# A hybrid decoder trunk on one core: the FFNs' gated values are transposed by VectorE and put in place through DRAM

## The chip, the cores and the metric

The kernel runs on one core of a Trainium2 chip. A core has engines with queues of their own: TensorE (PE, matmuls; PEld is its weight load), VectorE (DVE), ScalarE (ACT), GpSimd (POOL) and SyncE (SP), and 16 DMA engines that serve the DMAs which the engines' queues issue. Each queue runs its instructions in the order in which they stand; an instruction that waits holds all behind it. The metric is the time of one execution on the device, in microseconds.

## The reference

Two layers, on 256 tokens of width 1024, all in float32:

```
h += 1/2 * swiglu(rms_norm(h, ffn1_norm), w_gate, w_up, w_down)
h += W_out(sum of four gated token mixers of rms_norm(h))
h += cross_attention(rms_norm(h), rms_norm(mem))
h += 1/2 * swiglu(rms_norm(h, ffn2_norm), w_gate, w_up, w_down)
after the last layer: rms_norm(h, final_norm)

def swiglu(x, w_gate, w_up, w_down):
    return (jax.nn.silu(x @ w_gate) * (x @ w_up)) @ w_down
```

The change concerns the four FFNs (`swiglu`, hidden width 2816), the start of the first of them, and the final norm.

## The kernel before

Tokens are two blocks of 128 (`NB`), `b0` and `b1`. A float32 product is made of three products of rounded parts: weights are split in `wh` and `wl`, activations in `xh` and `xl` (or `hid`'s two parts), and TensorE adds wh·xh, wh·xl and wl·xh.

*Weights.* They come in chunks of 1 MB, four k-tiles of 128 x 512 columns. For each chunk `fetch` (L331) issues one load from SyncE's queue into `wr` (L343, three buffers), then in two halves ScalarE's rounding cast to `wh` (L350) and VectorE's residual `wl` (L351). `linear` (L367) uses a chunk with 24 matmuls: 12 for b0, 12 for b1, each 12 as four of wh·xh, four of wh·xl, four of wl·xh. So a first half of a cast serves the first two of every four.

*An FFN* (`ffn`, L538). The gate and up columns lie in 11 groups of 256 + 256 columns, each group two chunks; the first call of `linear` takes groups 0 and 1 together, in the order g0, g1, g0, g1 (chunks 0 to 3). At the end of a group, `evac` (L554) gates each block: ScalarE's Silu `sg` (L557), VectorE's product `toks` (L558), 128 tokens x 256 values. `hidden` (L541) then has TensorE transpose the four 128x128 squares into a PSUM bank `ht` (L547), and `split` (L364, L365) makes of it `hid`, hidden dimension on the partitions. After the 22 chunks of gate and up come 12 of the down product, which reads `hid`.

*The order.* TensorE's order is that of the program: work put off with `yield n` in a generator (`start`, `tick`) is taken up n half chunks later, so a group's transposes stand half a chunk to a chunk after its last matmul. The order of the other engines is made by a planner when the program is built, and is then fixed. `issue_after(x)` keeps an instruction behind x on its engine.

*The start.* The first chunks are loaded in pieces, then `arrive` (L1248) loads `h`. `tables` (L571) runs in the first FFN: it loads `pos`, `cst` and `bcs` from ScalarE's queue, makes sine tables `tab` (L608, L609) of angles `ang` that VectorE works out of `pos`, and a relative bias (`ge` and `bias`, L642, L644), whose parts fill VectorE through the first layer.

*The end.* `finish_` (L1218) makes, block by block, the second half's square sum on ScalarE, the variance `fvar` and GpSimd's power `rfin`, and scales the halves on ScalarE and VectorE (L1230, L1232).

Of the kernel before, what the change touches and what calls it, by code (L numbers as in the profile page):

```python
# [11 lines left out]
F32 = mybir.dt.float32  # L12
# [7 lines left out]
P = 128  # L20
# [132 lines left out]
def program(tc, a, out, upto="all"):  # L153
# [12 lines left out]
    fp = sb("fp", 2)  # L166
    sp = sb("sp", 4)
    mp = sb("mp", 11)
    lin = ctx.enter_context(tc.tile_pool(name="lin", bufs=4, space=PSUM))
    aux = ctx.enter_context(tc.tile_pool(name="aux", bufs=4, space=PSUM))  # L170
    ctx.enter_context(tc.manual_schedule(engines={mybir.EngineType.PE}))
# [364 lines left out]
        return evac  # L536

    def ffn(xT, nxt):  # L538
        hid = {}

        def hidden(g, toks):  # L541
            yield 2
            t4 = m4("hid", F32R).rearrange("p (s f t) -> p s f t", s=2, f=2)
            ps = bank("ht").rearrange("p (f t) -> p f t", f=2)
            for b in range(NB):
                for k in range(2):
                    pe.transpose(ps[:, k, blk(b)], toks[:, b, k * P:(k + 1) * P], ident)  # L547
            split(t4[:, 0], t4[:, 1], ps)
            hid[g] = t4

        def group(g):
            toks = f2("toks", "toks", 3).rearrange("p (b t) -> p b t", b=2)

            def evac(b, ps):  # L554
                nonlocal paced
                sg = fp.tile([P, 256], F32, tag="sg", name="sg")
                act.activation(sg, ps[:, :256], AF.Silu, scale=xT.r[:, b:b + 1])  # L557
                paced = dve.scalar_tensor_tensor(toks[:, b], ps[:, 256:], xT.r[:, b:b + 1], sg, ALU.mult, ALU.mult)  # L558
                if b == NB - 1:
                    start(hidden(g, toks))  # L560

            return evac

        linear(KD, 512, xT, [group(0), group(1)])
        for g in range(2, 11):
            linear(KD, 512, xT, [group(g)])
        for c in range(2):
            linear(KF, 512, lambda part, k: hid[k // 2][:, part, k % 2, :], [add_to_h(c, 0.5, nxt, 1 if c else 5)])


    def tables():  # L571
# [3 lines left out]
        with tc.issue_after(last.ins):  # L575
            act.dma_start(posi, a["pos"])
            act.dma_start(cst, a["consts"][:, P:CO["dec"][0]])
            act.dma_start(bcs, a["bcols"])
        act.activation(sel, C("sel")[:16], AF.Copy)
        yield 4  # L580
        for o, b, n in ((0, 0, 128), (128, 1, 256)):
            pool.tensor_tensor(reli[:, o:o + n], posi[:, b:b + 1].to_broadcast([P, n]), posi[:, NB:NB + n], ALU.subtract)
        dve.tensor_copy(relt, reli)
# [633 lines left out]
    def finish_(fn):  # L1217
# [3 lines left out]
        for b in range(NB):  # L1221
            square_sum(h[b][0], ss[:, b:b + 1])
            dve.tensor_tensor(t[b][:, :512], h[b][0], fn[:, :512], ALU.mult)
            dve.tensor_scalar(part[:, b:b + 1], ss[:, b:b + 1], 1.0 / D, EPS, ALU.mult, ALU.add)
        for b in range(NB):
            square_sum(h[b][1], ss[:, 2 + b:3 + b])
            v, r = small("fvar", 1), small("rfin", 1)
            dve.scalar_tensor_tensor(v, ss[:, 2 + b:3 + b], 1.0 / D, part[:, b:b + 1], ALU.mult, ALU.add)
            pool.tensor_tensor(r, v, mhalf[:, :1], ALU.pow)
            act.activation(t[b][:, :512], t[b][:, :512], AF.Copy, scale=r)  # L1230
            act.dma_start(out[blk(b), :512], t[b][:, :512])
            dve.scalar_tensor_tensor(t[b][:, 512:], h[b][1], r, fn[:, 512:], ALU.mult, ALU.mult)  # L1232
            nc.sync.dma_start(out[blk(b), 512:], t[b][:, 512:])

    def dump():
# [11 lines left out]

    def arrive():  # L1248
        yield 1
        for c in range(2):  # L1250
            for b in range(NB):
                nc.sync.dma_start(h[b][c], a["x"][b, :, c * 512:(c + 1) * 512])
# [41 lines left out]
```

## Time and profile before

| | |
|---|---|
| time, median of 3 runs | 1585.56 us (1585.09 to 1585.72) |
| the profiled execution | 1585.53 us |
| its span, first to last instruction | 1583.4 us |
| mean granted TensorE clock | 0.998 of full speed |
| busy: TensorE, VectorE, ScalarE | 1572.2, 1065.2, 830.2 us |
| `ht` on TensorE | 176 transposes, 26.3 us busy |
| casts `wh`, residuals `wl` | 536 each, 533.2 and 624.7 us busy |
| moved by DMA | 284.73 MB, 43153 packets, 4784 of them under 512 B |

Matmuls overlap in the pipeline, so the busy times of single ones add up to more than the time that they take in a row; the distance from start to start is what counts. A bracket after an instruction gives the time that the engine stood idle before it and the instruction that ended this.

### The profile page before, as it was taken

What the parts mean: (1) busy time and instruction counts of PE and PEld (TensorE: products, weight loads), DVE (VectorE), ACT (ScalarE), POOL (GpSimd) and SP (SyncE); (2) the same over time, 40 slices, a digit from 0 to 9 for tenths busy, and PEclk for the clock granted to TensorE, in tenths of its full rate; (3) what the DMA queues carried; (4) which work ended last, traced back from release to release, by engine and by line L of the source; (5) the groups of instructions that cost most, each with busy time, mean ns of one, the idle gap of its engine ahead of it and who ended that gap; (6) DMA issues with size and microseconds to landing.
All of it is one profiled execution on the core that took longest, in us unless ns stands there. A gap on an engine that the chain in (4) does not pass through costs nothing.

```text
span 1583.4 us, 20797 instructions
## 1 busy us (share of the span) xinstructions
PE 1572.2 (99%) x8208; PEld 1345.1 (85%) x8208; DVE 1065.2 (67%) x1704; ACT 830.2 (52%) x1236; POOL 26.0 (2%) x40
## 2 busy tenths in 40 slices
PE   9999999999999999999999999999999999999998
PEld 7888889898888988888888888898988899888886
DVE  5887699997787656554565546697656766565543
ACT  6744446566655545444454444475575555554443
POOL 0000000000000000000000000000000000000000
PEclk9999999999999999999999999999999999999999
DMA  7655544444655444555555556444546554455552
GB/s 291 239 180 179 194 169 160 165 164 144 212 214 177 169 160 163 187 182 182 191 188 188 183 176 209 151 159 157 184 149 237 186 186 164 156 182 176 191 174 74
DMA packets 43153, 284.73 MB, mean 180 GB/s; under 512 B 4784, under 2 KB 5168, under 8 KB 11056
## 3 DMA queue, kind: packets, MB, share of 16 engines
q1 hardware_dynamic: 40464, 276.12, 51.3%
q10 hardware_dynamic: 2592, 7.29, 1.4%
q8 instruction: 64, 1.05, 0.3%
q14 instruction: 33, 0.27, 0.0%
HBM read 282.34 MB, written 1.05 MB: 179 GB/s over the span
## 4 chain that ended last, share of the span: by engine, by line
PE 98%; DMA 1%; ACT 0%; DVE 0%; issue 0%; POOLq 0%; POOL 0%; ACTq 0%
PE lin L393 77%; PE lin L411 11%; PE tr L422 2%; PE ht L547 1%; PE xo L1191 1%; PE lin L381 1%; PE xs L1145 1%; DMA bcs<-bcols 1%; PE up L953 1%; PE my L869 0%; PE ds L1038 0%; PE ms L989 0%; PE pt L680 0%; DMA pcs<-pcols 0%; ACT wh L350 0%
## 5 line engine op out<-in xcount | busy, mean ns | idle before, releaser
L351 DVE TENSOR_TENSOR wl<-wr,wh 128x1024 fp32r<-128x1024 f32 (+3 forms) x536 | 624.7, 1191 | 375.1 <-ACT wh L350 372.7
L350 ACT ACTIVATE wh<-wr 128x1024 fp32r<-128x1024 f32 (+3 forms) x536 | 533.2, 1030 | 493.4 <-PE lin L393 381.7
L393 PE MATMUL lin<-wh,xh 128*128 128x512 f32 (+1 forms) x1200 | 328.5, 395 | 1.1 <-ACT wh L350 0.9
L393 PE MATMUL lin<-wl,xh 128*128 128x512 f32 (+1 forms) x1200 | 320.7, 389 | 0.6 <-DVE wl L351 0.6
L393 PE MATMUL lin<-wh,xl 128*128 128x512 f32 (+1 forms) x1200 | 320.4, 389 | 0.0
L393 PEld LDWEIGHTS lin<-wl,xh 128*128 128x128 f32 x1200 | 225.1, 188 | 48.0 <-DVE wl L351 1.4
L393 PEld LDWEIGHTS lin<-wh,xl 128*128 128x128 f32 x1200 | 225.3, 188 | 47.0
L393 PEld LDWEIGHTS lin<-wh,xh 128*128 128x128 f32 x1200 | 219.2, 188 | 43.7 <-ACT wh L350 2.2
L393 PE MATMUL lin<-wh,hid 128*128 128x512 f32 x704 | 176.0, 390 | 0.0
L393 PEld LDWEIGHTS lin<-wh,hid 128*128 128x128 f32 x704 | 131.6, 188 | 27.1
L393 PE MATMUL lin<-wl,hid 128*128 128x512 f32 x352 | 95.4, 389 | 0.0
L393 PEld LDWEIGHTS lin<-wl,hid 128*128 128x128 f32 x352 | 66.1, 188 | 13.9
L557 ACT ACTIVATE sg<-lin,rffn 128x256 f32<-128x256 f32 x88 | 40.9, 464 | 65.0 <-PE lin L393 63.7
L644 DVE SCALAR_TENSOR_TENSOR bias<-ge,d,bias 128x384 f32<-128x384 f32 x124 | 69.4, 610 | 0.3
L411 PE MATMUL lin<-xh,wh 128*128 128x256 f32 x384 | 62.0, 283 | 0.0
L558 DVE SCALAR_TENSOR_TENSOR toks<-lin,rffn,sg 128x256 f32<-128x256 f32 x88 | 42.3, 480 | 27.7 <-ACT sg L557 27.6
L411 PE MATMUL lin<-xh,wl 128*128 128x256 f32 x384 | 60.5, 279 | 0.0
L411 PE MATMUL lin<-xl,wh 128*128 128x256 f32 x384 | 60.5, 279 | 0.0
L411 PEld LDWEIGHTS lin<-xh,wh 128*128 128x128 f32 x384 | 52.0, 188 | 0.3
L411 PEld LDWEIGHTS lin<-xl,wh 128*128 128x128 f32 x384 | 51.7, 188 | 0.0
L411 PEld LDWEIGHTS lin<-xh,wl 128*128 128x128 f32 x384 | 51.7, 188 | 0.0
L444 ACT ACTIVATE junk<-h 128x512 bf16<-128x512 f32 x36 | 22.4, 623 | 30.6 <-DVE h L531 16.9
(395 smaller groups left out, 1559.4 us busy)
## 6 DMA issues: line engine op xcount, KB each, us to landing
wr<-gu SPq DMA_DIRECT2D x86, 1024.0 KB, 5.1
wr<-win SPq DMA_DIRECT2D x68, 1024.0 KB, 5.1
wr<-dn SPq DMA_DIRECT2D x40, 1024.0 KB, 4.9
wr<-wbr SPq DMA_DIRECT2D x16, 1024.0 KB, 4.9
wr<-w_out SPq DMA_DIRECT2D x8, 1024.0 KB, 5.2
wr<-xa_wk SPq DMA_DIRECT2D x8, 1024.0 KB, 4.9
wr<-xa_wq SPq DMA_DIRECT2D x8, 1024.0 KB, 4.9
wr<-xa_wv SPq DMA_DIRECT2D x8, 1024.0 KB, 5.0
```

The lines of the kernel that those rows point to most:

```text
L350: last = act.activation(hi[:, s], r[:, s], AF.Copy)
L351: dve.tensor_tensor(lo[:, s], r[:, s], hi[:, s].bitcast(F32), ALU.subtract)
L381: pe.matmul(p_[b][:, :n], lhsT=xT(part, k)[:, b * P:(b + 1) * P], rhs=w[:, k * n:(k + 1) * n], start=k == 0 and w is hi and part == 0, sto ...
L393: pe.matmul(p_[b][:, :n], lhsT=xT(part, k0 + k)[:, b * P:(b + 1) * P], rhs=w[:, k * n:(k + 1) * n], start=first, stop=last)
L411: pe.matmul(ps[i][:, j * 256:(j + 1) * 256], lhsT=ws[w][:, o:o + P], rhs=xT(part, k0 + k), start=k0 + k + part + w + j == 0, stop=k0 + k = ...
L422: pe.transpose(ps[:, k * P:(k + 1) * P], src[:, k * P:(k + 1) * P], ident)
L444: act.activation(j[:, :src.free_size()], src, AF.Square, accum_out=out_)
L547: pe.transpose(ps[:, k, blk(b)], toks[:, b, k * P:(k + 1) * P], ident)
L557: act.activation(sg, ps[:, :256], AF.Silu, scale=xT.r[:, b:b + 1])
L558: paced = dve.scalar_tensor_tensor(toks[:, b], ps[:, 256:], xT.r[:, b:b + 1], sg, ALU.mult, ALU.mult)
L644: dve.scalar_tensor_tensor(bias[:, hd], ge, d8[:, hd, i + 1:i + 2], bias[:, hd], ALU.mult, ALU.add)
L953: pe.matmul(ps[:, :n], lhsT=lowT[p_][:, k0 + k, blk(b)], rhs=wm[w][:, o + k * n:o + (k + 1) * n], start=i == 0, stop=i == len(seq) - 1)
```

## The change

In the FFNs, VectorE transposes each block of `toks` in squares of 32 x 32 into a tile `turned` (a `dve.transpose` with 128x8x32 elements, one per block, two per group), right after the gating. SyncE then issues four DMAs, one per 32 partitions, that write `turned` into a DRAM tile `rows` in runs of 256 B (64 KB each), and later one DMA that reads `rows` back as `hidt`, 256 KB. It waits for the writes to land. The split to `hid` now works on SBUF and in two pieces of 128x256. TensorE's transposes `ht` are gone; `linear` of the down product calls `hT`, which takes up a group's `hidden` if it isn't done. Three more edits: `tables` puts `sel` and all behind it off by eight half chunks in place of four behind `sel`; `arrive` calls `fetch()` before it loads `h`; and `finish_` makes both blocks' powers first, with VectorE's last products kept behind the second variance.

```diff
@@ -166,6 +166,7 @@
     fp = sb("fp", 2)
     sp = sb("sp", 4)
     mp = sb("mp", 11)
+    dp = ctx.enter_context(tc.tile_pool(name="dp", bufs=4, space=bass.MemoryType.DRAM))
     lin = ctx.enter_context(tc.tile_pool(name="lin", bufs=4, space=PSUM))
     aux = ctx.enter_context(tc.tile_pool(name="aux", bufs=4, space=PSUM))
     ctx.enter_context(tc.manual_schedule(engines={mybir.EngineType.PE}))
@@ -536,36 +537,51 @@
         return evac
 
     def ffn(xT, nxt):
-        hid = {}
-
-        def hidden(g, toks):
+        hid, started = {}, {}
+
+        def hidden(g, toks, turned):
+
+            rows = dp.tile([2 * P, 256], F32, tag="rows", name="rows")
+            w = rows.rearrange("(k j a) (i t) -> i a (k j) t", k=2, j=4, i=4)
+            r = turned.rearrange("p (k t) -> p k t", k=8)
+            for i in range(4):
+                nc.sync.dma_start(w[i], r[i * 32:(i + 1) * 32])
+            yield 1
+            t = f2("hidt", "half", 2)
+            nc.sync.dma_start(t.rearrange("p (k t) -> p k t", k=2), rows.rearrange("(k p) t -> p k t", k=2))
             yield 2
             t4 = m4("hid", F32R).rearrange("p (s f t) -> p s f t", s=2, f=2)
-            ps = bank("ht").rearrange("p (f t) -> p f t", f=2)
-            for b in range(NB):
-                for k in range(2):
-                    pe.transpose(ps[:, k, blk(b)], toks[:, b, k * P:(k + 1) * P], ident)
-            split(t4[:, 0], t4[:, 1], ps)
+            for f in range(2):
+                hi, lo = (x.rearrange("p (c i t) -> p c i t", c=2, i=4) for x in (t4[:, 0, f], t4[:, 1, f]))
+                split(hi, lo, t[:, f * 256:(f + 1) * 256].rearrange("p (i c t) -> p c i t", c=2, i=4))
             hid[g] = t4
 
         def group(g):
             toks = f2("toks", "toks", 3).rearrange("p (b t) -> p b t", b=2)
+            turned = f2("turned", "gate", 4)
 
             def evac(b, ps):
                 nonlocal paced
                 sg = fp.tile([P, 256], F32, tag="sg", name="sg")
                 act.activation(sg, ps[:, :256], AF.Silu, scale=xT.r[:, b:b + 1])
                 paced = dve.scalar_tensor_tensor(toks[:, b], ps[:, 256:], xT.r[:, b:b + 1], sg, ALU.mult, ALU.mult)
+                r = turned.rearrange("p (k j c t) -> p c k j t", j=4, k=2, c=2)[:, b]
+                dve.transpose(r, toks[:, b].rearrange("p (k j t) -> p k j t", k=2, j=4))
                 if b == NB - 1:
-                    start(hidden(g, toks))
+                    started[g] = start(hidden(g, toks, turned))
 
             return evac
 
         linear(KD, 512, xT, [group(0), group(1)])
         for g in range(2, 11):
             linear(KD, 512, xT, [group(g)])
+        def hT(part, k):
+            if k // 2 not in hid:
+                finish(started[k // 2])
+            return hid[k // 2][:, part, k % 2, :]
+
         for c in range(2):
-            linear(KF, 512, lambda part, k: hid[k // 2][:, part, k % 2, :], [add_to_h(c, 0.5, nxt, 1 if c else 5)])
+            linear(KF, 512, hT, [add_to_h(c, 0.5, nxt, 1 if c else 5)])
 
 
     def tables():
@@ -576,8 +592,8 @@
             act.dma_start(posi, a["pos"])
             act.dma_start(cst, a["consts"][:, P:CO["dec"][0]])
             act.dma_start(bcs, a["bcols"])
+        yield 8
         act.activation(sel, C("sel")[:16], AF.Copy)
-        yield 4
         for o, b, n in ((0, 0, 128), (128, 1, 256)):
             pool.tensor_tensor(reli[:, o:o + n], posi[:, b:b + 1].to_broadcast([P, n]), posi[:, NB:NB + n], ALU.subtract)
         dve.tensor_copy(relt, reli)
@@ -1222,14 +1238,19 @@
             square_sum(h[b][0], ss[:, b:b + 1])
             dve.tensor_tensor(t[b][:, :512], h[b][0], fn[:, :512], ALU.mult)
             dve.tensor_scalar(part[:, b:b + 1], ss[:, b:b + 1], 1.0 / D, EPS, ALU.mult, ALU.add)
+        r, got = [], []
         for b in range(NB):
             square_sum(h[b][1], ss[:, 2 + b:3 + b])
-            v, r = small("fvar", 1), small("rfin", 1)
-            dve.scalar_tensor_tensor(v, ss[:, 2 + b:3 + b], 1.0 / D, part[:, b:b + 1], ALU.mult, ALU.add)
-            pool.tensor_tensor(r, v, mhalf[:, :1], ALU.pow)
-            act.activation(t[b][:, :512], t[b][:, :512], AF.Copy, scale=r)
+            v = small("fvar", 1)
+            r.append(small("rfin", 1))
+            got.append(dve.scalar_tensor_tensor(v, ss[:, 2 + b:3 + b], 1.0 / D, part[:, b:b + 1], ALU.mult, ALU.add))
+            pool.tensor_tensor(r[b], v, mhalf[:, :1], ALU.pow)
+        for b in range(NB):
+            act.activation(t[b][:, :512], t[b][:, :512], AF.Copy, scale=r[b])
             act.dma_start(out[blk(b), :512], t[b][:, :512])
-            dve.scalar_tensor_tensor(t[b][:, 512:], h[b][1], r, fn[:, 512:], ALU.mult, ALU.mult)
+
+            with tc.issue_after(got[1].ins):
+                dve.scalar_tensor_tensor(t[b][:, 512:], h[b][1], r[b], fn[:, 512:], ALU.mult, ALU.mult)
             nc.sync.dma_start(out[blk(b), 512:], t[b][:, 512:])
 
     def dump():
@@ -1247,6 +1268,7 @@
 
     def arrive():
         yield 1
+        fetch()
         for c in range(2):
             for b in range(NB):
                 nc.sync.dma_start(h[b][c], a["x"][b, :, c * 512:(c + 1) * 512])
```

The names in what follows: a number behind a tile's name tells tiles of one name apart; `gu2` is the second FFN's gate and up matrix; line numbers of the changed kernel are one to some twenty higher.

TensorE in the second FFN, at the end of a group and the start of the next, before:

```order
L393 MATMUL lin_5963<-wh_6005,xl1_5561 128x512 x4
L393 MATMUL lin_5963<-wl_6006,xh1_5560 128x512 x4
L393 MATMUL lin_6043<-wh_6046,xh0_5496 128x512 x4
L393 MATMUL lin_6043<-wh_6046,xl0_5497 128x512 x4
L393 MATMUL lin_6043<-wl_6047,xh0_5496 128x512 x4
```

and now, at the end of the fifth group (`lin_5991` is its b1):

```order
L394 MATMUL lin_5991<-wh_6027,xh1_5641 128x512 x4
L394 MATMUL lin_5991<-wh_6027,xl1_5642 128x512 x4
L394 MATMUL lin_5991<-wl_6028,xh1_5641 128x512 x4
L394 MATMUL lin_6078<-wh_6081,xh0_5575 128x512 x4
L394 MATMUL lin_6078<-wh_6081,xl0_5576 128x512 x4
```

In both the next group's first chunk follows at once on the group's last matmul.

ScalarE around these chunks, before:

```order
L350 ACTIVATE wh_6046<-wr_6045 128x1024
L557 ACTIVATE sg_5958<-lin_5882,rffn2_5599 128x256
L350 ACTIVATE wh_6046<-wr_6045 128x1024
L350 ACTIVATE wh_6086<-wr_6085 128x1024 x2
L364 ACTIVATE hid_5996<-ht_5997 128x512
L557 ACTIVATE sg_6024<-lin_5962,rffn2_5599 128x256
L350 ACTIVATE wh_6127<-wr_6126 128x1024
L557 ACTIVATE sg_6039<-lin_5963,rffn2_5599 128x256
L350 ACTIVATE wh_6127<-wr_6126 128x1024
```

and now:

```order
L351 ACTIVATE wh_6027<-wr_6026 128x1024
L566 ACTIVATE sg_5979<-lin_5903,rffn2_5680 128x256
L566 ACTIVATE sg_6046<-lin_5990,rffn2_5680 128x256
L365 ACTIVATE hid_5962<-hidt_5924 128x256 x2
L566 ACTIVATE sg_6067<-lin_5991,rffn2_5680 128x256
L351 ACTIVATE wh_6081<-wr_6080 128x1024
L365 ACTIVATE hid_6050<-hidt_6012 128x256 x2
L351 ACTIVATE wh_6081<-wr_6080 128x1024
L351 ACTIVATE wh_6115<-wr_6114 128x1024 x2
```

The cast of the chunk that TensorE takes next (`wh_6046` before, `wh_6081` now) stood two Silus ahead of those of the group that ends there; now it stands behind both, with two pieces of `hid` between its halves.

SyncE from before the second FFN on, before:

```order
L343 DMA wr<-xa_wv 128x2048 x4
L343 DMA wr<-xa_wo 128x2048 x4
L343 DMA wr<-gu 128x2048 x22
L343 DMA wr<-dn 128x2048 x5
L343 DMA wr<-dn 128x1024
L343 DMA wr<-dn 128x2048 x5
```

and now, a part of the stretch of the 22 loads of gate and up:

```order
L344 DMA wr_6026<-gu2 128x2048
L551 DMA hidt_5836<-rows_5802 128x2x256
L548 DMA rows_5895<-turned_5808 32x8x64 x4
L548 DMA rows_5983<-turned_5901 32x8x64 x2
L551 DMA hidt_5924<-rows_5895 128x2x256
L548 DMA rows_5983<-turned_5901 32x8x64 x2
L344 DMA wr_6080<-gu2 128x2048
L551 DMA hidt_6012<-rows_5983 128x2x256
L548 DMA rows_6071<-turned_5989 32x8x64 x4
L344 DMA wr_6114<-gu2 128x2048
L551 DMA hidt_6100<-rows_6071 128x2x256
L344 DMA wr_6168<-gu2 128x2048
```

The loads of the FFN stood in one row; now four writes and a read of `rows` stand ahead of most of them.

ScalarE at the start, in the first FFN, before (`wh_419` is the cast of chunk 6, `wh_378` that of chunk 5):

```order
L350 ACTIVATE wh_333<-wr_332 128x1024 x2
L557 ACTIVATE sg_303<-lin_165,rffn1_263 128x256
L577 DMA cst_93<-consts 128x696
L578 DMA bcs_95<-bcols 128x688
L557 ACTIVATE sg_318<-lin_166,rffn1_263 128x256
L364 ACTIVATE hid_321<-ht_322 128x512
L576 DMA pos_364<-pos 128x258
L579 ACTIVATE sel_100<-cst_93 16x8
L350 ACTIVATE wh_378<-wr_377 128x1024 x2
L350 ACTIVATE wh_419<-wr_418 128x1024 x2
L350 ACTIVATE wh_462<-wr_461 128x1024 x2
L364 ACTIVATE hid_369<-ht_370 128x512
```

and now (`wh_443` is the cast of chunk 6):

```order
L592 DMA pos_384<-pos 128x258
L566 ACTIVATE sg_429<-lin_344,rffn1_275 128x256
L625 ACTIVATE tab_99<-ang_620 128x32
L625 ACTIVATE tab_99<-ang_620 128x16
L624 ACTIVATE tab_99<-angc_628 128x32
L624 ACTIVATE tab_99<-angc_628 128x16
L624 ACTIVATE tab_99<-angc_686 128x32
L625 ACTIVATE tab_99<-ang_678 128x32
L624 ACTIVATE tab_99<-angc_686 128x16
L625 ACTIVATE tab_99<-ang_678 128x16
L351 ACTIVATE wh_443<-wr_442 128x1024
L365 ACTIVATE hid_412<-hidt_370 128x256 x2
```

The cast of chunk 6 stood right behind two other casts and `sel`; now it stands behind the Silus of the chunk before, the issue of the `pos` load and the eight operations that make `tab`.

## Rows read from the trace of the kernel before

**Rows 1.** The page's chain that ended last, share of the span by engine
```profile
PE 98%; DMA 1%; ACT 0%; DVE 0%; issue 0%; POOLq 0%; POOL 0%; ACTq 0%
```

**Rows 2.** TensorE's waits; releaser, us in total, times, longest us
```profile
PE lin L393 <- ACT wh L350: 0.9, 1, 0.9
...
PE lin L393 <- DVE wl L351: 0.6, 2, 0.4
```

**Rows 3.** The chain in a last FFN stretch: start us, us, engine and line
```profile
1441.88 10.93 PE lin L393 x48
1452.81 0.44 PE ht L547 x4
```

**Rows 4.** ScalarE in that FFN: start us, us, instruction, idle before and releaser
```profile
1470.20 0.45 ACT L557 ACTIVATE sg<-lin,rffn 128x256 f32<-128x256 f32 x1
1470.56 1.05 ACT L350 ACTIVATE wh<-wr 128x1024 fp32r<-128x1024 f32 x1
```

**Rows 5.** The page's groups, VectorE: busy us, mean ns, idle before
```profile
L644 DVE SCALAR_TENSOR_TENSOR bias<-ge,d,bias 128x384 f32<-128x384 f32 x124 | 69.4, 610 | 0.3
...
L558 DVE SCALAR_TENSOR_TENSOR toks<-lin,rffn,sg 128x256 f32<-128x256 f32 x88 | 42.3, 480 | 27.7 <-ACT sg L557 27.6
```

**Rows 6.** DMA queues (packets, MB, share), then issues: KB each, us to landing
```profile
q1 hardware_dynamic: 40464, 276.12, 51.3%
q10 hardware_dynamic: 2592, 7.29, 1.4%
...
wr<-gu SPq DMA_DIRECT2D x86, 1024.0 KB, 5.1
...
out<-fin SPq DMA_DIRECT2D x2, 256.0 KB, 2.3
...
pos<-pos ACTq DMA_DIRECT2D x1, 129.0 KB, 6.1
pcs<-pcols ACTq DMA_DIRECT2D x1, 88.0 KB, 4.2
```

**Rows 7.** SyncE in the first microseconds: start us, us, DMA issue
```profile
6.77 0.43 SPq L1245 DMA_DIRECT2D xt<-xt  x1
```

**Rows 8.** TensorE in the first FFN, chunks 3 to 6, same columns
```profile
24.89 0.73 PE L393 MATMUL lin<-wh,xh 128*128 128x512 f32 x2 [0.93 <-ACT wh L350]
...
27.30 1.07 PE L393 MATMUL lin<-wh,xh 128*128 128x512 f32 x4
...
43.41 1.07 PE L393 MATMUL lin<-wh,xh 128*128 128x512 f32 x4
```

**Rows 9.** ScalarE in the first FFN, same columns
```profile
27.50 0.48 ACT L557 ACTIVATE sg<-lin,rffn 128x256 f32<-128x256 f32 x1 [0.76 <-PE lin L393]
...
41.39 1.28 ACT L620 ACT_TABLE_LOAD   x1
```

**Rows 10.** VectorE in the first FFN, where it waits for a table load
```profile
35.00 0.23 DVE L632 COPY bias<-cst 128x128 f32<-128x128 f32 x1 [3.79 <-DMA cst<-consts]
...
35.74 0.28 DVE L633 COPY bias<-cst 128x256 f32<-128x256 f32 x1
...
37.29 5.03 DVE L351 TENSOR_TENSOR wl<-wr,wh 128x1024 fp32r<-128x1024 f32 x4
```

**Rows 11.** VectorE in the first FFN, the small angle operations
```profile
50.24 0.18 DVE L602 TENSOR_SCALAR angk<-angc 128x48 f32<-128x48 f32 x1
50.33 0.18 DVE L606 TENSOR_SCALAR ang<-ang 128x48 f32<-128x48 f32 x1
```

**Rows 12.** Windows at the end: busy us by engine (x count), granted clock, DMA
```profile
1576.00:1579.00 3.00, 0.00 (x0) 0.00 (x0) 1.67 (x5) 1.60 (x5) 1.10 (x2) 0.87 0.01 4
1579.00:1583.00 4.00, 0.00 (x0) 0.00 (x0) 0.59 (x1) 0.56 (x1) 0.00 (x0) 0.50 0.71 259
```

**Rows 13.** VectorE at the end, start us, us, instruction
```profile
1577.35 0.75 DVE L1232 SCALAR_TENSOR_TENSOR fin<-h,rfin,bias 128x512 f32<-128x512 f32 x1 [0.66 <-POOL rfin L1229]
...
1578.84 0.75 DVE L1232 SCALAR_TENSOR_TENSOR fin<-h,rfin,bias 128x512 f32<-128x512 f32 x1 [0.67 <-POOL rfin L1229]
```

## The prediction

> **What bounds the kernel now.** I read the chain of work that ended last first: TensorE holds 98% of it [rows 1]. So a change is worth what it takes from TensorE's queue, less what it makes TensorE wait. The list of TensorE's waits says how little slack is lost today: one wait of 0.9 us for ScalarE's cast and two, 0.6 us in all, for VectorE's residual in this matmul line [rows 2]. Third, the chain in a late FFN gives the grain: a group is 48 matmuls in 10.93 us, then four transposes in 0.44 [rows 3]. A chunk (24 matmuls, half a group) is therefore 5.47 us at 0.228 us a matmul, and its first 12 serve block 0.
>
> The one place where casts are late today shows what lateness costs, and how. At 24.89 TensorE waits for the second half of a cast [rows 8]; in the order of ScalarE that half stood behind the Silu of the chunk that TensorE had just finished. A Silu can't start before TensorE ends its half chunk (27.30 against 27.50, a lag of 0.2 us [rows 8, 9]), so a cast queued behind it is late whatever its data did. This is the pattern that I look for in the new order.
>
> **The change, part by part.** Sums are made against the profiled execution, 1585.53 us (1583.4 of span and 2.1 around it), which is the median of the runs within 0.04.
>
> *Removed.* 44 sets of four transposes at 0.44 us, all in TensorE's chain [rows 3]. Three of them lie in the stretch that I rebuild below, so 41 x 0.435 = **-17.8 us**.
>
> *Added beside TensorE.* Per group VectorE gets two block transposes of 128x256. None is in this trace; bounds are a copy of that size at 0.28 us [rows 10] and the 128x384 two-operand row at 0.61 [rows 5]; I take 0.48, the 128x256 gating row [rows 5], nearest in size and form. The split in two pieces adds some 0.2 us on ScalarE and VectorE each. All that fits beside the casts, four halves of 1.05 us on ScalarE [rows 4] and four of about 1.2 on VectorE [rows 10] in a group's 10.9 us: it costs nothing itself, and where it stands in the queues does.
>
> *The order of the queues.* SyncE, which issued nothing but weights through an FFN, now waits in line for transposes and for landings, five issues of 0.43 us [rows 7] per group, with the next weight load behind them. So loads come later, and the planner has put casts later on ScalarE. In each of the FFNs two to four I find two places (the eleventh and nineteenth chunk of gate and up, the first of them printed with the change) where both halves of a cast stand behind the last Silu of the chunk that TensorE ends just before. Let T be that end. Silu starts at T+0.2; the cast follows 0.36 later [rows 4] and takes 1.05, to T+1.6; two splits of `hid` at about 0.4 (a 128x256 pass of ScalarE takes 0.45 [rows 4]) and the second half end at T+3.4. Two matmuls use the first half, 22 need the second: 3.4 + 22 x 0.228 = 8.4 instead of 5.5, **2.9 us lost**. The next chunk's load stands behind the four writes of the group that ended at T: gating 0.48, transpose 0.48 after the Silu of 0.47, then 4 x 0.43, so issue at T+3.35, landing 5.1 later [rows 6] at T+8.45, halves cast at 9.5 and 10.5, TensorE through at 15.5 instead of 8.4 + 5.5: **1.6 more** (0 if the load overlaps better). 6 places x 4.5 = **+27.2 us**, bounds 17.4 to 27.2. What hides the other groups is a lead of a chunk or more in the order.
>
> *First FFN, steady part.* At chunks 14 and 20 the cast has the same place, and VectorE has in addition four bias products of 0.61 us [rows 5] ahead of the residual; with them, the block's transposition and the splits its second half ends some 7 us after T; 14 matmuls (3.2 us) remain: 10.1 instead of 5.5, 4.6 each. Chunks 16 and 22 have only the second half behind a Silu: 1.2 each, like today's 0.9 [rows 2]. **+11.6**, bounds 8.2 (no VectorE term: 2 x 2.9 + 2 x 1.2) and 11.6.
>
> *Start.* The extra early load takes today's stall at 24.89 away. But in the new order the residual of chunk 5 stands behind five copies that wait for the `cst` load, which lands at 35.00 [rows 10], and its issue keeps its place. Copies to 35.8, two halves at 1.2 us to 38.1, 14 matmuls: chunk 5 ends at 41.3 (43.41 today [rows 8]). The cast of chunk 6 is the worst place: ahead of it on ScalarE stand a table load of 1.28 us [rows 9], Silu, two splits, the issue of the `pos` load, and eight sine operations that need it. Table load from 39.9 (its inputs follow chunk 5's residual), Silu 0.36 and splits 0.8: `pos` is issued at 42.4. Its landing is 6.1 us today behind two larger loads, 4.2 for a load of 88 KB, 2.3 for the output [rows 6]; nearest in size and unhindered is 4.2: 46.6. VectorE then runs 26 small operations at 0.1 [rows 11] and one cast, to 49.5; the weight cast ends at 50.75, its second half after the splits at 52.55, chunk 6 at 57.55, chunk 7 at 63.0. Today chunk 7 ends at 43.41 + 5.45 + 0.44 + 5.45 = 54.75. **+8.2**, bounds 6.3 and 10.1 by the `pos` landing.
>
> *Clock.* TensorE stands idle some 9 us there. At the kernel's end, where it has no matmul, the granted clock falls to a mean of 0.87 in the first three microseconds and 0.50 (1.2 of 2.4 GHz) after [rows 12]. So chunk 6 may start at the lower level; no row shows how long it stays. Bounds: nothing, and a whole chunk at half speed, 5.5 us. I take **+2**.
>
> The Trainium skill (TensorE: Matmul & The Clock Gate, Part 1) says that the low level is the default and that activity releases it, which fits rows 12; by it a low stretch after that idle time is sure, and the sum would only move within the bounds just given.
>
> *End.* Both variances now come before the last two products. Today the second product starts at 1578.84, 1.49 after the first [rows 13]; now they follow one another at their own length, 0.75 [rows 13], the first some 0.25 later: **-0.5**, bounds -1 and 0.
>
> Sum: 1585.5 - 17.8 + 27.2 + 11.6 + 8.2 + 2 - 0.5 = **1616 us**. With the lower bounds 1585.5 - 17.8 + 17.4 + 8.2 + 6.3 - 1 = 1599, with the upper 1622, and 1635 with the small packets' price below on top.
>
> The Trainium skill has a rule against the move itself (VectorE: DVE Perf Modes, Rules for kernel authors): a whole 128x128 transposition belongs on TensorE where its result may lie in PSUM, since VectorE's is one of 32x32 blocks only. Here TensorE's costs 0.44 us a group of the engine that bounds the kernel [rows 3], so by that price alone the move would gain 19 us; the rule speaks of one operation's cost, and the sum above loses by what surrounds it.
>
> **Rivals.** *Small packets.* The four writes are 1024 packets of 256 B a group, 64 for each of 16 DMA engines, ahead of weights in the same queue. Two queues fit 0.32 us per packet of 6.8 KB and 0.137 per packet of 2.8 KB (share x span x 16 / packets [rows 6]), hence about 0.02 us for one of 256 B: 1.3 us a group, or +13 in ten places (the six, and four of the first FFN). Were each to cost as much as the mean packet of the second queue, it is 64 x 0.137 = 8.8 us a group, 88 in the ten places: 1704. For it: no row shows packets as small as these in number; against it: the fit.
>
> The Trainium skill (DMA: Bandwidth & Descriptors, Specifications) asks for 512 B or more per packet and says that below it a read-modify-write is done; if that doubles the fitted 1.3 us, the ten places give +26, not 88, and the time is 1642.
>
> *Half of the places hold.* If in the six places the loads come earlier than I think and TensorE waits for a second half only (1.3 us each, as in today's stall), they cost 8: 1585.5 - 17.8 + 8 + 11.6 + 8.2 - 0.5 = 1595.
>
> *Faster: the casts are in time.* If TensorE reaches these chunks late or the casts early enough, only the gain is left: 1585.5 - 19.1 - 0.5 = 1566, and 1574 with the start's 8. For it: neither VectorE nor ScalarE is near its limit, and today's order costs TensorE 1.5 us in all [rows 2]. Against it: the lag of a Silu is physical, and a first-in queue can't bring a cast ahead of it. It decides where all stalls together stay under 18.3 us; I count 49.
>
> *The change doesn't do what it says*: excluded, since the new order of TensorE has none of the 176 transposes.
>
> **How the numbers follow.** Forecast 1616: 0.72, with its own range of 1599 to 1635. Half of the places: 0.09. Small packets at the high price: 0.06. Faster: 0.11. A balance within 0.2% by smaller stalls: 0.02. Range 1594 to 1640: it takes in the forecast and the half case, allows the packets half as much again as fitted, and leaves out faster, the high packet price and the balance, 0.19. About 0.2% (3.2 us) is what a measurement of this kernel can tell from no change; faster 0.11, same 0.02, slower 0.87.
>
> **What would show it.** Right: no `ht` on TensorE; in its waits some 15 to 20 new entries for the cast and the residual, 40 to 50 us in all, with pairs of about 3 and 1.5 us in each FFN; one stall of 7 to 10 us near 42 us, and a lower granted clock behind it; SyncE's waits on the transpose or on the landing of `rows`; `pos` landing some 4 us after its issue. Wrong: TensorE's waits at a few us (then the leads were longer than I read), weight loads landing much later than 5.1 us (then it is the packets), or VectorE transposes of over 1 us, by which the casts of every group would slip.

## The result, and the profile after

The changed kernel takes **1625.03 us** in the median of its runs (1621.71 to 1628.21; one disturbed run is left out of the comparison), beside 1585.28 for the kernel before on the same chip: a ratio of **1.0249, interval 1.0237 to 1.0261**. The profiled execution took 1624.99, its span 1622.9 against 1583.4.

The page of the kernel after: busy time of the engines, the chain that ended last (which answers to [rows 1]), the new transpose, and the DMA lines that answer to [rows 6].

```profile
PE 1574.8 (97%) x8032; PEld 1336.5 (82%) x8032; DVE 1103.9 (68%) x1836; ACT 831.5 (51%) x1277; POOL 26.5 (2%) x40
...
PE 91%; DMA 3%; DVE 2%; ACT 2%; SPq 1%; issue 1%; POOL 0%; POOLq 0%; DVEq 0%; ACTq 0%
...
L569 DVE STREAM_TRANSPOSE turned<-toks 128x256 f32<-128x256 f32 x88 | 38.9, 442 | 1.9
...
q1 hardware_dynamic: 100304, 299.20, 55.7%
...
wr<-gu SPq DMA_DIRECT2D x86, 1024.0 KB, 5.4
...
rows<-turned SPq DMA_DIRECT2D x176, 64.0 KB, 1.9
hidt<-rows SPq DMA_DIRECT2D x44, 256.0 KB, 4.6
```

TensorE kept 98% of the chain before and keeps 91% now; the weight loads of the FFNs, VectorE, the casts and SyncE's writes have taken most of the rest. Its waits in the kernel after (engine, line and releaser; us in total, times, longest), which answer to [rows 2]:

```profile
PE lin L394 <- ACT wh L351: 33.3, 26, 6.6
PE lin L394 <- DVE wl L352: 3.1, 4, 1.1
PE rowp L512 <- DVE dg L511: 2.3, 1, 2.3
```

The cast's wait has grown from 0.9 us, once, to 33.3 us, 26 times. One wait is new and was not forecast: `rowp`, a small product of the memory norm, 2.3 us in the first mixer.

Where the stalls sit is read on TensorE in the second FFN, around the eleventh chunk of gate and up (start us, us, instruction, idle before and its releaser):

```profile
682.56 0.73 PE L394 MATMUL lin<-wh,xh 128*128 128x512 f32 x2 [1.73 <-ACT wh L351]
684.12 0.73 PE L394 MATMUL lin<-wh,xh 128*128 128x512 f32 x2 [0.83 <-ACT wh L351]
...
690.93 0.73 PE L394 MATMUL lin<-wh,xh 128*128 128x512 f32 x2 [1.53 <-ACT wh L351]
691.88 0.73 PE L394 MATMUL lin<-wh,xh 128*128 128x512 f32 x2 [0.22 <-ACT wh L351]
692.46 1.87 PE L394 MATMUL lin<-wh,xl 128*128 128x512 f32 x4
```

ScalarE there:

```profile
680.87 0.47 ACT L566 ACTIVATE sg<-lin,rffn 128x256 f32<-128x256 f32 x1 [1.63 <-PE lin L394]
681.45 1.06 ACT L351 ACTIVATE wh<-wr 128x1024 fp32r<-128x1024 f32 x1
682.41 0.71 ACT L365 ACTIVATE hid<-hidt 128x256 fp32r<-128x256 f32 x2
683.03 1.04 ACT L351 ACTIVATE wh<-wr 128x1024 fp32r<-128x1024 f32 x1
...
689.83 2.00 ACT L351 ACTIVATE wh<-wr 128x1024 fp32r<-128x1024 f32 x2 [5.76 <-DMA wr<-gu]
```

And SyncE's queue:

```profile
682.37 1.82 SPq L548 DMA_DIRECT2D rows<-turned  x4
684.23 0.46 SPq L344 DMA_DIRECT2D wr<-gu  x1
```

TensorE ends the tenth chunk at T = 680.67. Silu starts 0.20 later, the cast 0.78 after T, two pieces of `hid` stand between the cast's halves, and TensorE waits twice. The four writes leave SyncE only once the transposes are there, the next weight load is issued at T + 3.56, it lands where the next cast begins (689.83), and TensorE waits for that cast too. This is the picture of the prediction, and its times hold within some 0.2 us up to the issue of that load; the cast behind it begins at T + 9.16, where the landing was forecast for T + 8.45.

One thing in it is not ScalarE's order. At the eleventh chunk the cast also waits for its own load, which stood on SyncE's queue behind a read and two writes. ScalarE at this chunk in the fourth FFN:

```profile
1477.73 0.47 ACT L566 ACTIVATE sg<-lin,rffn 128x256 f32<-128x256 f32 x1 [1.63 <-PE lin L394]
1479.54 1.06 ACT L351 ACTIVATE wh<-wr 128x1024 fp32r<-128x1024 f32 x1 [1.33 <-DMA wr<-gu]
```

At the nineteenth chunk the cast starts 0.37 us after the Silu does, its load landed more than 2 us before. Here it starts 1.81 after it, in the third FFN 0.81 and in the second 0.58. So in three of the six places the load is late too. The chain of work that ended last, from 660 to 770 us (the second FFN), also goes through loads:

```profile
by line: PE lin L394 80.1%; DMA wr<-gu 10.0%; ACT wh L351 3.7%; SPq L548 3.1%; DVE toks L567 0.9%; ACT sg L566 0.9%; DVE turned L569 0.8%; issue 0.6%
```

It runs twice from TensorE over Silu, gating, transpose, the four writes and the load behind them to the next cast.

TensorE, then ScalarE, at the start (chunk 6 of the first FFN, same columns):

```profile
46.66 1.22 PE L394 MATMUL lin<-wh,xh 128*128 128x512 f32 x2 [6.55 <-ACT wh L351]
48.22 1.22 PE L394 MATMUL lin<-wh,xh 128*128 128x512 f32 x2 [0.34 <-ACT wh L351]
```

```profile
37.92 0.33 ACTq L592 DMA_DIRECT2D pos<-pos  x1
...
45.57 1.04 ACT L351 ACTIVATE wh<-wr 128x1024 fp32r<-128x1024 f32 x1
```

The chain of angle operations, sines and cast is there, and its stall is the longest of the run; the `pos` load that was to lead it lands just before VectorE is free for the angles (more on this below). And the clock, in windows of the same execution (window and its length; busy us of PE, PEld, DVE, ACT, POOL with counts; granted clock; DMA share, GB/s):

```profile
46.00:50.00 4.00, 3.00 (x6) 1.99 (x7) 3.03 (x4) 2.96 (x5) 0.00 (x0) 0.50 1.00 369
...
692.00:696.00 4.00, 4.00 (x11) 3.14 (x12) 3.17 (x5) 1.51 (x3) 0.00 (x0) 0.57 1.01 403
876.00:880.00 4.00, 2.92 (x7) 1.84 (x8) 3.09 (x5) 2.02 (x4) 0.00 (x0) 0.60 0.68 109
880.00:884.00 4.00, 4.00 (x12) 3.14 (x11) 0.00 (x0) 0.83 (x1) 0.00 (x0) 0.55 0.98 341
```

After a stall or a pair of them TensorE works at the lower of its two levels (1.2 of 2.4 GHz) for some microseconds: from 692 to 696 it is busy throughout at 0.57, so it loses 4 x 0.43 = 1.7 us without being idle. Eight such stretches cost some 16.5 us, worked out the same way; no row of waits holds them.

Where the time came from, by milestones (the start of the same instruction in both traces, near the end of each FFN, mixer and cross-attention; us):

| stretch | after less before | predicted |
|---|---|---|
| first FFN, with the start | +15.70 | +18.3 |
| first mixer | +3.83 | 0 |
| second, third, fourth FFN | +6.98, +5.76, +6.96 | +4.3 each |
| second mixer, both cross-attentions | 0.0 | 0 |
| final norm | +0.24 | -0.5 |
| span | +39.5 | +30.6 |

### The profile page after: what moved, and what is told of

Read it like the earlier page. It is cut to its first block, busy times and chain, and to the rows that moved or that the text cites. A ratio compares the mean times of both kernels' runs of the same rounds, so it can differ in the third digit from the quotient of the medians.

```text
span 1622.9 us, 20951 instructions
## 1 busy us (share of the span) xinstructions
PE 1574.8 (97%) x8032; PEld 1336.5 (82%) x8032; DVE 1103.9 (68%) x1836; ACT 831.5 (51%) x1277; POOL 26.5 (2%) x40
## 3 DMA queue, kind: packets, MB, share of 16 engines
q1 hardware_dynamic: 100304, 299.20, 55.7%
## 4 chain that ended last, share of the span: by engine, by line
PE 91%; DMA 3%; DVE 2%; ACT 2%; SPq 1%; issue 1%; POOL 0%; POOLq 0%; DVEq 0%; ACTq 0%
PE lin L394 71%; PE lin L412 11%; DMA wr<-gu 3%; PE tr L423 2%; ACT wh L351 1%; SPq L548 1%; PE xo L1207 1%; PE xs L1161 1%; PE lin L382 1%; PE up L969 1%; DVE wl L352 1%; PE my L885 0%; PE ds L1054 0%; DVE bias L660 0%; PE ms L1005 0%
## 5 line engine op out<-in xcount | busy, mean ns | idle before, releaser
L394 PE MATMUL lin<-wh,xh 128*128 128x512 f32 (+1 forms) x1200 | 333.9, 399 | 32.2 <-ACT wh L351 32.2
L394 PE MATMUL lin<-wl,xh 128*128 128x512 f32 (+1 forms) x1200 | 325.7, 393 | 3.1 <-DVE wl L352 3.1
L394 PE MATMUL lin<-wh,xl 128*128 128x512 f32 (+1 forms) x1200 | 326.1, 394 | 0.0
L394 PEld LDWEIGHTS lin<-wh,xh 128*128 128x128 f32 x1200 | 223.8, 191 | 88.4 <-ACT wh L351 44.4
L394 PEld LDWEIGHTS lin<-wl,xh 128*128 128x128 f32 x1200 | 228.8, 191 | 52.0 <-DVE wl L352 4.8
L394 PEld LDWEIGHTS lin<-wh,xl 128*128 128x128 f32 x1200 | 228.8, 191 | 47.8
L569 DVE STREAM_TRANSPOSE turned<-toks 128x256 f32<-128x256 f32 x88 | 38.9, 442 | 1.9
```

Of the source, the lines that this page charges most:

```text
L394: pe.matmul(p_[b][:, :n], lhsT=xT(part, k0 + k)[:, b * P:(b + 1) * P], rhs=w[:, k * n:(k + 1) * n], start=first, stop=last)
L569: dve.transpose(r, toks[:, b].rearrange("p (k j t) -> p k j t", k=2, j=4))
```

## The experiments

The theory: the transposition without TensorE is a gain, and all of the loss is the order of the queues. Casts stand behind the last Silu, and weight loads behind writes that wait for a transpose. Rivals: the DRAM trip itself (45,056 packets of 256 B), VectorE's transposes, or the start's reordering.

**No trip through DRAM** (`notrip`).

```diff
-            rows = dp.tile([2 * P, 256], F32, tag="rows", name="rows")
-            w = rows.rearrange("(k j a) (i t) -> i a (k j) t", k=2, j=4, i=4)
-            r = turned.rearrange("p (k t) -> p k t", k=8)
-            for i in range(4):
-                nc.sync.dma_start(w[i], r[i * 32:(i + 1) * 32])
-            yield 1
-            t = f2("hidt", "half", 2)
-            nc.sync.dma_start(t.rearrange("p (k t) -> p k t", k=2), rows.rearrange("(k p) t -> p k t", k=2))
-            yield 2
+            yield 3
+            t = turned
```

> The changed kernel without the way through DRAM: VectorE's 32x32 transposes and the two-piece split stay, the split reads the block-transposed tile itself, and the four writes and the read are left out (so the hidden values lie in wrong places). My theory, that the loss comes from SyncE's queue (writes and reads ahead of weight loads, and casts planned late for that): no stall in the FFNs is left; 1585.3 - 19.1 (transposes) - 3.0 (two stalls of the old start) + 3.8 (the wait for dg in the first mixer and the low clock behind it) = 1567, TensorE's waits under 6 us. Rival, VectorE's transposes or the split in pieces hold up the casts: 1600 or more, with the stalls at the eleventh and nineteenth chunk still there.

Measured: 1565.30 us, ratio 0.9873 [0.9859, 0.9888]. VectorE's transposes are all there, so they are not the cost. The late FFNs take 5.35 us less than before, each.

**The trip on GpSimd's queue** (`poolq`): the same five DMAs per group, issued by an engine that has little else to do (the `...` stand for the two views, which stay as they are).

```diff
-                nc.sync.dma_start(w[i], r[i * 32:(i + 1) * 32])
+                nc.gpsimd.dma_start(w[i], r[i * 32:(i + 1) * 32])
-            nc.sync.dma_start(t..., rows...)
+            nc.gpsimd.dma_start(t..., rows...)
```

> The changed kernel with the writes and reads of rows issued from GpSimd's queue in place of SyncE's; all else the same. If the place in SyncE's queue is the cause: about 1567, as without the way through DRAM, with the same packets moved. Rival, the traffic of small packets (256 B) is what makes weights late: the stalls stay, about 1620, and weight loads land later than 5.4 us. Second rival, GpSimd issues so slowly that hid is late at the down product: waits of several us at the first down chunks, 1575 to 1590.

Measured: 1564.53 us, 0.9870 [0.9855, 0.9884]. The whole trip costs nothing on that queue. Its only waits of TensorE over 0.3 us are `rowp` (2.3 us) and one of 1.1 at the start, while SyncE's queue holds nothing but weights in the same stretch of time:

```profile
663.46 27.92 SPq L344 DMA_DIRECT2D wr<-gu  x6
```

But this edit changes more than the queue. The page shows that this queue moves the same bytes in far fewer packets, and that a write lands later (4.4 us, 1.9 on SyncE's):

```profile
q0 software_dynamic: 9152, 23.08, 4.2%
...
rows<-turned POOLq DMA_DIRECT2D x176, 64.0 KB, 4.4
```

So small packets were still a rival, and the next runs take the two apart.

**Only the writes, only the read** (`wpool`, `rpool`): one of the two lines of the diff above in each.

> The changed kernel with only the four writes of each group issued from GpSimd's queue; the read of rows stays on SyncE's. If it is the writes, which wait for the transposes with weight loads behind them, that cost the time: 1563 to 1567, no stall at the eleventh and nineteenth chunk. Rival, the read, which waits for the writes to land with weight loads behind it, carries a good part: 1580 to 1605.

> The mirror image: the writes stay on SyncE's queue, the read goes to GpSimd's. If the writes cost the time: stalls of 2 to 6 us in all FFNs as in the changed kernel; the order has even more casts (four a late FFN, the whole chunk each) behind the Silu of the chunk just ended, so 1625 to 1650. Rival, the read carries the cost: 1565 to 1590.

Measured: 1563.53 us, 0.9864 [0.9849, 0.9878], with the writes on GpSimd's queue; 1627.11 us, 1.0265 [1.025, 1.028], with the read there. So it is the writes on SyncE's queue, with the order that the planner makes for them, and the read with its wait for their landing costs nothing on either queue. TensorE's waits with the read alone on GpSimd's queue:

```profile
PE lin L394 <- ACT wh L351: 37.4, 19, 6.8
```

**The same bytes in runs of 2 KB** (`bigpk`), on SyncE's queue.

```diff
-            w = rows.rearrange("(k j a) (i t) -> i a (k j) t", k=2, j=4, i=4)
-            r = turned.rearrange("p (k t) -> p k t", k=8)
+            w = rows.rearrange("(i p two) t -> i p (two t)", i=4, two=2)
+            r = turned
```

> The changed kernel with writes of rows in runs of 2 KB per partition in place of eight of 256 B (the values then lie in wrong places in rows; as many bytes, as many DMAs, all on SyncE's queue). The planner puts these writes at other places, and no cast of the FFNs stands behind the Silu of the chunk just ended. If that order is what costs: 1563 to 1570, even with writes and reads in SyncE's queue. Rival, waits in SyncE's queue cost by themselves, whatever the planned order: 1600 to 1625, with late weight loads.

Measured: 1567.16 us, 0.9886 [0.9871, 0.9901]. By itself this looks like proof for the packets. It isn't: the planner sets another order for this form, in which hardly a cast stands late (TensorE waits 0.9 and 0.7 us in that line, both in the first FFN), so packets and order changed together. It needed a run that changes the order and leaves the packets.

**The writes put off** (`late6`): SyncE's queue and the 256 B runs as in the change, one line more.

```diff
+            yield 6
             for i in range(4):
                 nc.sync.dma_start(w[i], r[i * 32:(i + 1) * 32])
```

> The changed kernel with one line more: each group's writes are put off by six half chunks (yield 6). Writes and read stay on SyncE's queue, with the same 256 B runs, bytes and count. In the order that the planner then makes, no cast of the FFNs stands behind the Silu of the chunk just ended. If that order is the cause: 1563 to 1567, TensorE's waits under 6 us, with as many packets as the changed kernel. Rival, the small packets on the hardware's queue cost by themselves: 1600 or more, in spite of the better order.

Measured: 1572.98 us, 0.9923 [0.9908, 0.9938], 6 to 10 us above what I expected. The queue's line on the page, then TensorE's waits:

```profile
q1 hardware_dynamic: 100304, 299.20, 58.0%
```

```profile
PE lin L394 <- ACT wh L351: 3.2, 2, 3.0
PE lin L394 <- DVE wl L352: 3.0, 6, 1.4
```

The packets are the 100,304 of the change, and the waits for the cast are 3.2 us, not 33.3. The second FFN takes 190.26 us by its milestones, 190.25 in `wpool`, where the writes go in merged packets: **in the late FFNs the small packets cost nothing**. Nor does waiting in SyncE's queue by itself: in all, its writes wait for transposes for 199.9 us here and for 177.8 in the kernel after. But the load behind them is now that of the fourth chunk to come, not of the second, and so has time. The miss lies in the first FFN, 8.7 us longer than in `wpool`, and all before 145 us. TensorE at its first place there:

```profile
43.11 0.73 PE L394 MATMUL lin<-wh,xh 128*128 128x512 f32 x2 [3.03 <-ACT wh L351]
```

Through this FFN ScalarE and VectorE also carry the tables and the bias products, and the new order is tight at other points: here ScalarE waits 3.68 us for the `bcs` load to land, with the sines and the cast behind it, and later residuals stand behind bias products. I had counted only the places of the change.

**The writes put off by less** (`late3`): `yield 3` in the same place.

> The same with the writes put off by three half chunks. The order then has more late casts than the changed kernel: in each late FFN three chunks whose whole cast stands behind the Silu of the chunk just ended, and two with the second half. If the order is the cause: three x 2.4 + two x 1.1 a late FFN and low clock behind them, so no better than the changed kernel, 1625 to 1645. Rival, putting writes off helps by itself (they wait less in SyncE's queue): between 1570 and 1615.

Measured: 1625.22 us, 1.0249 [1.0233, 1.0264]. TensorE's waits:

```profile
PE lin L394 <- ACT wh L351: 33.3, 32, 4.8
```

As many microseconds as in the change, in more and shorter pieces. The chain that ended last, from 660 to 770 us (the second FFN), where it went through loads in the kernel after:

```profile
by line: PE lin L394 90.8%; ACT wh L351 7.1%; ACT sg L567 1.3%; issue 0.9%
```

It goes from TensorE to Silu to cast and back, and the same holds in the third and fourth FFN: no load is on it. By milestones these three FFNs lose 33.9 us against FFNs without a stall, 35.8 in the kernel after. So casts in these places are enough for the loss, loads in time or not. Putting the writes off isn't a dial: at three half chunks the planner's order still has casts right behind the last Silu, at six TensorE waits for none of them in the late FFNs.

**The start and the end alone** (`startfinish`): the kernel before, with the edits to `arrive`, `tables` and `finish_`, TensorE's transposes kept.

> The kernel before with only the edits of arrive, tables and finish_. My theory: the start's two stalls go (-3.0), the first mixer gets the 2.3 us wait for dg and a low clock behind it (+3.8), the end moves by 0 to -0.5: 1585.3 to 1586.3, the same. Rival, the start edits carry the stall of 6.6 us at chunk 6: 1590 to 1595.

Measured: 1586.45 us, 1.0007 [0.9997, 1.0016]. By milestones the start gains 2.4 us, the first mixer loses 3.85, and the end loses 0.09. The loss is the same new stall as after, and what follows it at the lower clock:

```profile
454.63 0.78 PE L511 MATMUL rowp<-dg,cst 128*128 128x128 f32 x4 [2.34 <-DVE dg L510]
455.07 2.05 PE L393 MATMUL lin<-wh,xh 128*128 128x512 f32 x4
```

So these edits, not the transposition, put the memory norm's small chain late in the first mixer; and at the start the long stall of the kernel after comes only together with the new transposition.

**The gap filled** (`filler`): 13 matmuls that nobody reads (1.71 us) ahead of the eleventh and the nineteenth chunk in FFNs two to four.

```diff
         for g in range(2, 11):
+            if g in fillers:
+                wm = bank("warm")
+                for i in range(13):
+                    pe.matmul(wm[:, :256], lhsT=xT(0, 0)[:, :P], rhs=xT(0, 0), start=True, stop=True)
             linear(KD, 512, xT, [group(g)])
```

> The changed kernel with 13 matmuls of 128x256 (1.5 us, results unused) put on TensorE before the eleventh and nineteenth chunk of FFNs two to four, where it stands idle 1.5 us or more anyway; all other orders are the same. If the granted clock falls because TensorE idles there: the clock stays at 1.00 in those places, and 8 to 11 us of the 1625 come back, 1614 to 1617. Rival, the clock's falls have another cause: 1625, with the same low stretches. If the added matmuls aren't hidden in the idle time: up to 9 us more, 1634.

Measured: 1627.66 us, 1.0265 [1.0249, 1.028]: a miss of 10 us and more, and the run that taught most on the clock. In the third FFN, windows, then TensorE:

```profile
876.00:880.00 4.00, 2.61 (x17) 1.94 (x15) 2.45 (x5) 3.09 (x5) 0.00 (x0) 1.00 0.50 117
880.00:884.00 4.00, 3.94 (x17) 3.27 (x18) 1.51 (x3) 0.01 (x1) 0.00 (x0) 1.00 0.92 244
```

```profile
876.17 1.71 PE L580 MATMUL warm<-xh 128*128 128x256 f32 x13
878.50 0.73 PE L394 MATMUL lin<-wh,xh 128*128 128x512 f32 x2 [0.61 <-ACT wh L351]
880.06 0.73 PE L394 MATMUL lin<-wh,xh 128*128 128x512 f32 x2 [0.83 <-ACT wh L351]
...
886.60 0.73 PE L394 MATMUL lin<-wh,xh 128*128 128x512 f32 x2 [1.24 <-ACT wh L351]
```

The clock stays at 1.00 where it was 0.60 and 0.55. But TensorE then reaches the next chunk sooner, and finds its cast late (1.24 at 886.60, which the kernel after doesn't show at this chunk), and in three of the six places the clock falls later instead (0.71 at 936 to 940). A cast that waits for its load sets the end of these two chunks, whichever way TensorE spends the time before it. In the three FFNs the low clock cost some 5 us instead of 11, yet the six places together still cost 36.1 us by milestones, 35.8 in the kernel after. (The first FFN, which has no filler, took 3.3 us more than in the profiled execution of after.)

**The best version** (`poolfix`, and `late6fix` as its likeness on SyncE's queue): `poolq` or `late6`, with the memory norm's row put off.

```diff
             act.dma_start(mt[c], a["memt"][:, c * 1024:(c + 1) * 1024])
-        yield 2
+        yield 4
         ps = row_bank(rm)
```

> The version with writes and reads on GpSimd's queue, and TensorE's rowp product of the mixers' memory norm put off by two more half chunks, against the wait of 2.3 us for dg in the first layer. Theory: that wait goes and nothing else moves, 1561 to 1563 (1564.5 - 2.3, and up to 1.6 of low clock less). Rival, another wait takes its place: 1564 to 1566.

> Writes put off by six half chunks, and the memory norm's rowp product by two more, all on SyncE's queue. Theory: the wait of 2.3 us in the first mixer goes and nothing else changes: 1560 to 1563, as the version on GpSimd's queue.

Measured: `poolfix` 1561.29 us, **0.9847 [0.983, 0.9863]**, the fastest and 24 us below the kernel before; TensorE's longest wait in it is 1.1 us, at the start. `late6fix` 1571.04 us, 0.9907 [0.989, 0.9923]: the `rowp` wait is gone, but the 3.3 us stall at 43.11 and the others of the first FFN stay, and I had expected 1560 to 1563.

## Why the prediction was right

The time, 1625, lies in the range, 9 us above the forecast, and slower was the sign. Point by point:

- **The pattern: right.** A cast that stands behind the last Silu of the chunk just ended is late; all 36.4 us of waits for cast and residual lie in places that were named, the six of the late FFNs and five of the first. That this order, and neither the transposes nor the bytes, is the cause is shown by `wpool` and `late6`, where the late casts are gone, by another queue or by one `yield`, and the loss turns into a gain, and by `late3`, where late casts alone bring the loss. What the prediction didn't see: at the eleventh chunk the load is late as well, not only at the chunk behind it.
- **Removed: a little low.** 0.435 us a group was taken; a late FFN without a stall (`notrip`) gains 5.35, 0.486 a group. VectorE's transpose took 0.44 us, 0.48 was taken; it costs nothing, as said.
- **The six places: the mis-sized term.** They cost 6.98 + 5.76 + 6.96 + 3 x 5.35 = 35.8 us, 6.0 each where 4.5 was forecast. The listed idle time is 19.6 us in 18 stalls, and a pair of matmuls after a stall takes 0.73 us where it takes 0.46 in a stream, some 5 more. The other 11.2 are TensorE at 1.2 GHz, of which the sum had nothing in these places. The follow-on loss of 1.6 for the next chunk's load is there as idle time in the second FFN (1.53 and 1.60); in the third and fourth, where the chunk before it ran slowly, it is 0.21 or nothing. `filler` shows that the two replace one another: the late load sets the end of these two chunks, and the clock only decides which row shows it.
- **First FFN, steady part: right in kind, a little low.** Chunks 14 and 20 lose 3.9 us idle each (1.51, 0.82, 0.47 and 1.07 in one) where 4.6 was forecast, chunks 16 and 22 1.06 each where 1.2 was. That is 9.9. With 1.7 of low clock behind chunk 20 and some 2.8 for the pairs after the ten stalls it is 14.4, from start to start, where +11.6 was forecast: the sum counted neither. The bias products ahead of the residual are in it as the waits on `wl`.
- **Start: the cast's place right, the size too high, and not by the `pos` landing.** Chunk 7 ends 5.2 us later, 8.2 and 2 for the clock were forecast. The `pos` load landed in 3.4 us (4.2 taken) and was issued at 37.92, not 42.4, since chunk 5 was not held: `cst`, issued earlier, landed in 3.0 us. TensorE was through with chunk 5 at 39.95 (41.3 forecast). GpSimd, which waits for `pos`, then VectorE's first angle operation:

```profile
41.36 0.97 POOL L598 TENSOR_TENSOR pos<-pos 128x128 int32<-128x128 int32 x2 [16.28 <-DMA pos<-pos]
41.68 0.12 DVE L602 CAST posf<-pos 128x2 f32<-128x2 int32 x1
```

VectorE comes to the angles straight from gating and transposing chunk 5, 0.3 us after `pos` is there. So its own work set the start of the angles, and the forecast's bounds, which hung on the landing, were set by the wrong term.

- **The clock: right in kind, far too small.** +2 at the start was 1.9. But the clock fell after shorter stalls as well, seven more times, for some 15 us in all. The rows of before had no stall within a stretch of matmuls above 0.93 us, and I took the one place whose stall looked like the kernel's end. By the Trainium skill (TensorE: Matmul & The Clock Gate, Part 1) the low level is the default; the 0.50 at 46 to 50 us agrees.
- **First mixer: missed.** +3.83, 2.34 idle and 1.5 at the low clock. The start's edits were followed to the end of chunk 7 only, and `startfinish` shows that they reach further.
- **End: missed in sign.** The products did move together, but the second power took longer. GpSimd and VectorE at the end of the kernel after, answering to [rows 13]:

```profile
1616.00 0.55 POOL L1247 TENSOR_TENSOR rfin<-fvar,mhalf 128x1 f32<-128x1 f32 x1 [189.70 <-DVE fvar L1246]
1616.78 0.75 DVE L1253 SCALAR_TENSOR_TENSOR fin<-h,rfin,bias 128x512 f32<-128x512 f32 x1
1616.94 1.00 POOL L1247 TENSOR_TENSOR rfin<-fvar,mhalf 128x1 f32<-128x1 f32 x1 [0.39 <-DVE fvar L1246]
...
1617.97 0.75 DVE L1253 SCALAR_TENSOR_TENSOR fin<-h,rfin,bias 128x512 f32<-128x512 f32 x1 [0.45 <-POOL rfin L1247]
```

The second product starts 1.19 us after the first (1.49 before, 0.75 forecast), for it waits for a power of 1.00 us; the first starts later, and nothing is left.

- **The rivals.** Small packets: the extra 59,840 packets on q1 (the read's are among them) took (0.557 x 1622.9 - 0.513 x 1583.4) x 16 / 59,840 = 0.0245 us each, 0.02 was fitted; and `late6` shows that they cost no time in the late FFNs. The Trainium skill (DMA: Bandwidth & Descriptors, Specifications) asks for 512 B or more; in `late6`, whose queue q1 takes 0.58 of the DMA engines' span with them, the late FFNs show no price for less. Faster: it had 0.11, and it is where the kernel goes as soon as the casts are in time: 1566 was worked out, 1561 to 1565 measured. The Trainium skill's rule (VectorE: DVE Perf Modes, Rules for kernel authors) for TensorE's transposition did not hold in this kernel, which TensorE bounds: 1563.53 us without it, 1585.52 with it.

That the total came within 9 us is in part luck: the start was 5.0 us too dear and the removal 2.1 too small, while the late places were 8.6, the mixer 3.8, the first FFN's steady part 2.8 and the end 0.7 too cheap.

Open: why the planner gives the casts these places with the writes on SyncE's queue and not on GpSimd's. Its prices are no part of the trace, and `late3` shows that a small shift doesn't take it out of this order. `late3` shows that late casts cost this much with no load on the chain; whether late weight loads alone, with the casts in their good places, would cost anything was not tried.

## What to carry to other kernels

When work is taken off the engine that is the bound, look first at what the move puts into the issue queues and, behind that, at where the planner then places the work that feeds the bound: here a gain of 22 us and a loss of 40 differ only in the queue of four writes and in the order that the planner made for each. Look for each operation that feeds TensorE and stands, in its engine's row, behind something that waits for the chunk TensorE is just ending. Price a stall with what follows it, a stretch at the lower clock and the next load that is late too, and check a price by a run that changes the order and keeps the bytes.

## What the runs showed of the hardware

- The clock can fall after stalls that are short and split, and the same stalls don't always bring it down: 1.51 and 0.82 us at 925.56 are followed by 0.57 (928 to 932), the same 1.51 and 0.82 at 732.91 by 1.00 (734 to 746). No row here tells the two apart.
- The time of the kernel after spreads, 1621.7 to 1628.2 us, where the kernel before stays within 1.0 us; what makes the spread is not shown.
- A tiny power on GpSimd (128x1) took 1.00 us beside VectorE's 128x512 product of two tiles, 0.55 alone; the same in `poolq` and `startfinish` (0.99).
- The same DMAs were moved in 9,152 packets when GpSimd issued them, 59,840 when SyncE did, and a 64 KB write then took 4.4 us to land instead of 1.9.
